# The down product of a hybrid decoder layer: 18 of its 22 features by seven block products in place of eight

## The chip, the cores and the metric

One core of a Trainium2 chip runs the whole layer in one launch. The metric is the device time in microseconds of one execution; the kernel before and the kernel after are run on the same chip. The five engines of the core work by their own queues: TensorE (PE) multiplies matrices, VectorE (DVE), ScalarE (ACT) and GpSimd (POOL) work element by element, and SyncE (SP) issues nearly all DMAs.

## What is computed

One layer for 1024 prompt tokens and 8 sampling tokens (1032 columns, kept as features x tokens), width 1024, feed-forward width 2816, all in float32:

```
def swiglu(x, w_in, w_out):
    gate, up = jnp.split(x @ w_in, 2, axis=-1)
    return (jax.nn.silu(gate) * up) @ w_out
...
x = x + 0.5 * swiglu(rmsnorm(x, ffn1_norm_g), ffn1_w_in, ffn1_w_out)
mix, ... = token_mix(rmsnorm(x, mix_norm_g), ...)
x = x + mix
x = x + 0.5 * swiglu(rmsnorm(x, ffn2_norm_g), ffn2_w_in, ffn2_w_out)
```

The change is in the product with `w_out` of both feed-forward blocks, here called the down product; that with `w_in` is called the up product.

## The kernel before

Everything is cut into tiles of 128 rows: 8 row tiles of the width, 22 of the feed-forward width (called features, `NF`). Each float32 operand is split into a high part (a cast to fp32r on ScalarE) and a low part (operand minus high part, mostly on VectorE; `split`, L250), and each product is three matmuls: high by high, high by low, low by high (`mm3`, L319).

*Up product* (`ffn_in`, L651). From the fifth feature on (the fourth in the second block) it is done by seven block products in place of eight (Strassen's scheme in Winograd's form): the reduction is halved, gate and up are the two halves of one side, and two column blocks of 258 are the other, for two column halves p. Seven operands of the tokens (`xT`) stay for all features; seven of the weights per feature (`w_ops`, L478) are made from two loads, with four additions on GpSimd, a cast on ScalarE and a subtraction on VectorE each. Results go to `hd` in DRAM.

*Down product* (`ffn_out`, L706). It runs plainly in five groups of features (`KGROUPS`, L37), each over 8 row tiles m and 3 column chunks of 344: `one` (L709) does 3 matmuls per feature into a PSUM bank `mm`, and then VectorE adds half the bank to the row tile `x` (the residual). Hidden tiles come back from `hd` by `h_tile` (L677: a load of 1032 columns, a cast, a subtraction). Weights come through `issue` (L296) into eight reserved slots, which `reserve` (L279) claims in the last feature of the up product. In the last group the order is turned, chunk by chunk, so that the work after it (`last_cb`, the next norm's squares and splits) can start on the first chunk.

*Order.* Of the instructions only those of PE stand in the order in which the code records them; the other engines' are put in order by a scheduler when the kernel is built. All large tiles are taken from 44 slots of 1060 columns (`SLOTS`). Work that is made ahead is written as generators (`builders`): `adv` (L418) lets each take a step after a row tile's chunk or a product, and a generator waits (`room`, L414) while too few slots are free. `need_op` (L514) steps them until the operand exists.

Of the kernel before, what the change touches and what calls it, by code (L numbers as in the profile page):

```python
# [36 lines left out]
KGROUPS = [(0, 4), (4, 4), (8, 6), (14, 4), (18, 4)]  # L37
# [77 lines left out]
class Net:  # L115
    def __init__(self, tc, ctx, io):
# [17 lines left out]
        self.alive = 0  # L134
# [120 lines left out]
    def make_plan(self):  # L255
# [12 lines left out]
        for o, w in zip(out, (io["w_out1"], io["w_out2"])):  # L268
            for f0, g in KGROUPS:
                per = PER[g]  # L270
                o += [(w[m0:m0 + per, :, f0:f0 + g, :].rearrange("m p f c -> p m (f c)"), [per, g * P], None) for m0 in range(0, KT, per)]
# [206 lines left out]
    def w_ops(self, s1, s2, n, out, limit):  # L478
# [4 lines left out]
        r1, r2 = self.bt([P, 2 * n], s="r1"), self.bt([P, 2 * n], s="r2")  # L483
        nc.sync.dma_start(r1, s1)
# [13 lines left out]
        st = self.bt([P, 2 * n], s="ws")  # L498
        tt(st[:, a], r2[:, a], r2[:, b], ALU.add)
# [8 lines left out]
        self.fr(r2)  # L508
        tt(r1[:, b], r1[:, b], st[:, b], ALU.subtract)
        self.fr(st)  # L510
        yield from op(r1[:, b])
        self.fr(r1)

# [137 lines left out]
    def ffn_in(self, xT, hd, tail, head):  # L651
# [3 lines left out]
        for f, ps in steps:  # L655
# [5 lines left out]
            for i in range(7):  # L661
# [12 lines left out]
                if f == NF - 1 and i == 1:  # L674
                    self.reserve()
# [9 lines left out]
    def out_ops(self, hd, get):  # L685

        self.hs, self.xr = [], []

        def gen():
            for f in range(NF):  # L690
                while f > 1 and not self.plan and not self.live:
                    yield False
                yield from self.room(3, 2)
                self.hs.append(self.h_tile(f, hd))
                yield True
                if f == KGROUPS[0][1] - 1:
                    for m in range(KT):
                        yield from self.room(1, 2)
                        x = self.bt(s="x")
                        self.nc.sync.dma_start(x, get(m))  # L700
                        self.xr.append(x)
                        yield True

        self.builders.append(gen())

    def ffn_out(self, last_cb):  # L706
        nc = self.nc

        def one(m, c0, w, whi, wlo, o, f0, g):  # L709
            ps = self.pmm()  # L710
            s = slice(c0, c0 + w)
            for j in range(g):
                ks = slice(o + j * P, o + (j + 1) * P)
                h = self.need_op(self.hs, f0 + j)
                self.mm3(ps, whi[:, ks], wlo[:, ks], h[0][:, s], h[1][:, s], j == 0, j == g - 1)
            x = self.need_op(self.xr, m)
            nc.vector.scalar_tensor_tensor(x[:, s], ps, 0.5, x[:, s], ALU.mult, ALU.add)
            self.adv()

        for f0, g in KGROUPS:  # L720
            per = PER[g]
            if f0 + g < NF:
                for m0 in range(0, KT, per):
                    whi, wlo = self.take()
                    for m in range(m0, m0 + per):
                        for c0, w in CHUNKS:
                            one(m, c0, w, whi, wlo, (m - m0) * g * P, f0, g)
                    self.drop()
            else:
                wide = [(self.bt([P, per * g * P], F32R, "whi"), self.bt([P, per * g * P], F32R, "wlo")) for _ in range(KT // per - 3)]  # L730
                ws = [self.take() for _ in range(3)]
                for t in wide:
                    ws.append(self.extra(*t))
                acc = self.bt(s="acc")
                for c0, w in CHUNKS:
                    for m in range(KT):
                        whi, wlo = ws[m // per]
                        one(m, c0, w, whi, wlo, (m % per) * g * P, f0, g)
                        last_cb(self.xr, m, c0, w, None)
                        self.square(acc[:, c0:c0 + w], m, self.xr[m][:, c0:c0 + w])  # L740
# [6 lines left out]
            for f in range(f0, f0 + g):  # L747
                self.fr(*self.hs[f])
# [1010 lines left out]
```

## Time and profile before

| | us |
|---|---|
| median of 3 runs | 2116.67 (2114.20 to 2116.69) |
| profiled execution, its own time | 2115.43 |
| its span, first to last instruction | 2113.2 |
| first block: head and up product | 8.7 to 509.0 |
| first block: down product | 508.9 to 758.5 |
| token mixing and its output product | 758.4 to 1376.3 |
| second block: head and up product | 1376.2 to 1846.7 |
| second block: down product | 1846.6 to 2098.6 |

The profile is of one execution. A row of the groups gives line, engine, operation, written and read tiles, shapes and count, then the busy time and the mean ns of one, then the idle time of the engine just before them and what ended it. Nearly all element-wise work has line L89, that of a helper that records it, so the tiles tell it apart: `wop` is a weight operand, `xlo`/`hlo`/`lo` are low parts, `sw` is the SwiGLU's tile, `ws` and `r` are sums and raw tiles of weights. In a row by windows the columns are named in its header; PEclk is the clock that TensorE was granted, as a share of full speed. In a row of the timeline the first two numbers are start and duration in us.

### The profile page before, as it was taken

How to read it: one execution, taken by the hardware profiler on the slowest of the kernel's cores; microseconds unless marked ns; L12 is line 12 of the kernel's file. 1: busy time of each engine (PE TensorE's matmuls, PEld its weight loads, DVE VectorE, ACT ScalarE, POOL GpSimd, SP SyncE). 2: the span in 40 equal slices, each digit the busy share in tenths (PEclk: the TensorE clock that was granted, in tenths of full speed). 3: DMA queues.
4: the chain of work that ended last, by engine and by line, in shares of the span. 5: the costliest groups of instructions: out<-in, count | busy, mean ns of one | idle time of the engine just before them, and what ended most of it. 6: DMA issues, size and time to landing. Idle time of an engine off the chain costs nothing.

```text
span 2113.2 us, 37138 instructions
## 1 busy us (share of the span) xinstructions
PE 2024.6 (96%) x15062; PEld 1963.6 (93%) x15062; DVE 1222.1 (58%) x2624; ACT 699.8 (33%) x1491; POOL 594.9 (28%) x517
## 2 busy tenths in 40 slices
PE   7799999999999999999999979999999999999997
PEld 6799999999999998787888869899999999999997
DVE  7755555555533544676977874685555555464335
ACT  5233333333211333545243332443333333331112
POOL 3354444341000131332211111245444444200003
PEclk7999999999999999999999979999999999999999
DMA  4112222227322221211212151221222222552112
GB/s 152 60 58 91 81 73 84 86 71 281 113 68 60 84 81 35 69 45 32 67 46 50 57 181 35 97 70 61 86 81 83 79 81 76 194 195 84 55 41 81
DMA packets 109771, 180.81 MB, mean 86 GB/s; under 512 B 35168, under 2 KB 63744, under 8 KB 109584
## 3 DMA queue, kind: packets, MB, share of 16 engines
q1 hardware_dynamic: 109568, 178.41, 26.6%
q8 instruction: 118, 1.93, 0.4%
q14 instruction: 53, 0.43, 0.1%
q0 software_dynamic: 32, 0.03, 0.0%
HBM read 135.60 MB, written 43.85 MB: 85 GB/s over the span
## 4 chain that ended last, share of the span: by engine, by line
PE 40%; DVE 8%; DMA 1%; issue 1%; SPq 1%; ACT 0%; POOL 0%; DVEq 0%; ACTq 0%; POOLq 0%
PE mm L321 6%; PE mm L322 6%; PE mm L323 6%; PE ps L528 4%; PE ps L530 4%; PE ps L529 4%; PE ps L243 3%; PE mm L528 2%; PE mm L530 2%; PE mm L529 2%; DVE conv L89 1%; DVE inv L89 1%; SPq L102 1%; DVE Tb L89 1%; DVE x L89 1%
## 5 line engine op out<-in xcount | busy, mean ns | idle before, releaser
L528 PE MATMUL ps<-xhi,wop 128*128 128x258 f32 x1480 | 421.0, 284 | 7.4 <-DVE sw L89 7.2
L530 PE MATMUL ps<-xhi,wop 128*128 128x258 f32 x1480 | 419.3, 283 | 0.0
L529 PE MATMUL ps<-xlo,wop 128*128 128x258 f32 x1480 | 419.3, 283 | 0.0
L321 PE MATMUL mm<-hhi,hi 128*128 128x344 f32 x1008 | 322.3, 320 | 0.0
L322 PE MATMUL mm<-hlo,hi 128*128 128x344 f32 x1008 | 322.3, 320 | 0.0
L323 PE MATMUL mm<-hhi,lo 128*128 128x344 f32 x1008 | 321.6, 319 | 0.0
L89 DVE TENSOR_TENSOR wop<-r,wop 128x512 fp32r<-128x512 f32 x185 | 158.5, 859 | 253.9 <-ACT wop L89 239.8
L528 PEld LDWEIGHTS ps<-xhi,wop 128*128 128x128 f32 x1480 | 280.9, 190 | 8.7 <-issue 7.2
L529 PEld LDWEIGHTS ps<-xlo,wop 128*128 128x128 f32 x1480 | 281.9, 191 | 0.0
L530 PEld LDWEIGHTS ps<-xhi,wop 128*128 128x128 f32 x1480 | 281.2, 190 | 0.0
L89 DVE SCALAR_TENSOR_TENSOR x<-mm,x 128x344 f32<-128x344 f32 x240 | 123.3, 515 | 220.0 <-PE mm L323 217.9
L89 ACT CAST hi<-raw 128x1024 fp32r<-128x1024 f32 (+1 forms) x78 | 76.7, 984 | 357.0 <-PE mm L322 327.0
L321 PEld LDWEIGHTS mm<-hhi,hi 128*128 128x128 f32 x1008 | 189.4, 188 | 0.3 <-DVE x L89 0.3
L323 PEld LDWEIGHTS mm<-hhi,lo 128*128 128x128 f32 x1008 | 189.4, 188 | 0.0
L322 PEld LDWEIGHTS mm<-hlo,hi 128*128 128x128 f32 x1008 | 189.3, 188 | 0.0
L89 POOL TENSOR_TENSOR acc<-acc,t 128x344 f32<-128x344 f32 (+1 forms) x50 | 45.5, 911 | 508.2 <-ACT t L89 495.9
L321 PE MATMUL mm<-xnhi,hi 128*128 128x344 f32 x488 | 172.1, 353 | 0.0
L528 PE MATMUL mm<-xhi,wop 128*128 128x258 f32 x592 | 167.5, 283 | 0.0
L530 PE MATMUL mm<-xhi,wop 128*128 128x258 f32 x592 | 167.2, 283 | 0.0
L529 PE MATMUL mm<-xlo,wop 128*128 128x258 f32 x592 | 167.0, 282 | 0.0
L89 ACT CAST wop<-r 128x512 fp32r<-128x512 f32 x185 | 114.7, 621 | 144.6 <-PE mm L530 77.0
L323 PE MATMUL mm<-xnhi,lo 128*128 128x344 f32 x488 | 158.6, 325 | 0.0
(320 smaller groups left out, 4607.5 us busy)
## 6 DMA issues: line engine op xcount, KB each, us to landing
r<-in_w_in SPq DMA_DIRECT2D x86, 512.0 KB, 3.6
hraw<-hd SPq DMA_DIRECT2D x44, 516.0 KB, 5.0
hd<-sw SPq DMA_DIRECT2D x74, 258.0 KB, 2.0
raw<-in_w_out SPq DMA_DIRECT2D x34, 512.0 KB, 4.0
raw<-in_w_mix SPq DMA_DIRECT2D x22, 512.0 KB, 3.6
raw<-in_w_out SPq DMA_DIRECT2D x24, 384.0 KB, 3.2
x<-in_x SPq DMA_DIRECT2D x16, 516.0 KB, 9.0
xd<-x SPq DMA_DIRECT2D x24, 172.0 KB, 1.9
```

The source lines that it names most:

```text
L89: return fn(out, *a, **k)
L102: return self.eng.dma_start(out, src)
L243: self.nc.tensor.matmul(out, lhsT, rhs, start=start, stop=stop)
L321: mm(ps, whi, xhi, start=start, stop=False)
L322: mm(ps, whi, xlo, start=False, stop=False)
L323: mm(ps, wlo, xhi, start=False, stop=stop)
L528: mm(ps, w[:, a], x[0][:, c], start=first, stop=False, skip_group_check=True)
L529: mm(ps, w[:, a], x[1][:, c], start=False, stop=False, skip_group_check=True)
L530: mm(ps, wlo, x[0][:, c], start=False, stop=last, skip_group_check=True)
```

## The change

Features 0 to 17 of the down product are done by seven block products, in three groups of six features (`SGROUPS`, `KG` = 3 features in each half of the reduction). Row tiles go in four pairs; a pair, the two halves of the features and two column blocks of 258 make one scheme of seven products, done for both column halves p. One such pass over 14 products is called a cycle here; a group is four cycles. Each product is nine matmuls of 258 columns (`out_product`). Products are accumulated in three PSUM banks so that after each one VectorE adds half of a bank to one block of `x` (`OUT_BANK`, `OUT_TO`): 14 evictions of 258 columns per cycle.

The operands are made by two generators. `wb_ops` makes seven weight operands of 384 columns per cycle, with four additions on GpSimd; at most four are alive (`B_LIVE`). `h_ops` loads eight raw tiles of 774 columns per group and makes seven hidden operands for each p, in three slots per index: a cast of 774 columns, subtractions of 258 and 516 columns on VectorE, and eight subtractions of 774 columns on GpSimd in all. A group's hidden operands stay through its four cycles and are freed index by index in the last. The last four features are done as the last group was before, with three takes and one wide tile; the slots for that are reserved in the last cycle of the third group, no more in the up product. Both blocks are changed alike; the token mixing is not touched.

The core of the diff (the loops that pass arguments on are left out):

```diff
-KGROUPS = [(0, 4), (4, 4), (8, 6), (14, 4), (18, 4)]
+KG = 3
+SGROUPS = [f * 2 * KG for f in range(3)]
+REST = len(SGROUPS) * 2 * KG
+OUT_BANK = (0, 1, 0, 2, 0, 1, 0)
+OUT_TO = ((0, 0), (1, 1), (0, 1), (0, 0), (1, 1), (0, 1), (1, 0))
+B_LIVE = 4
...
+    def wb_ops(self, s1, s2, n, out, limit):
...
+        def op(x):
+            while self.alive >= limit() or not self.slots:
+                yield False
+            t = self.bt([P, 2 * n], F32R, "wop")
+            self.alive += 1
+            self.split(t[:, a], t[:, b], x)
+            out.append(t)
+            yield True
+
+        yield from op(r1[:, a])
...
+        tt(st[:, a], r2[:, a], r2[:, b], ALU.add)
+        tt(st[:, b], st[:, a], r1[:, a], ALU.subtract)
+        tt(r2[:, a], r1[:, a], r2[:, a], ALU.subtract)
...
-                if f == NF - 1 and i == 1:
-                    self.reserve()
...
+    def h_ops(self, hd, f0, out, more):
...
+        for i in range(7):
+            yield from room(3)
+            ts = [self.bt([P, 4 * HW], F32R, "hop") for _ in range(3)]
+            views = []
+            for p, r in enumerate(raws):
+                t = (0, 0)
+                if i in (1, 2):
+                    tt(r[t], r[(0, 1) if i == 1 else (1, 1)], r[t], ALU.subtract)
+                elif i == 4:
+                    tt(r[0, 1], r[1, 1], r[0, 1], ALU.subtract)
+                elif i == 6:
+                    tt(r[1, 0], r[1, 0], r[t], ALU.subtract)
+                x = r[(t, t, t, (1, 0), (0, 1), (1, 1), (1, 0))[i]]
+                hi, lo = ts[p][:, :n], [ts[p][:, n:], ts[2][:, p * e:(p + 1) * e]]
+                self.nc.scalar.copy(hi, x)
+                f = hi.bitcast(F32)
+                self.nc.vector.tensor_tensor(lo[0], x[:, :HW], f[:, :HW], ALU.subtract)
+                self.nc.vector.tensor_tensor(lo[1], x[:, HW:], f[:, HW:], ALU.subtract)
...
+    def out_product(self, i, w, x, banks):
...
+        for k in range(KG):
+            a, b = w[:, k * P:(k + 1) * P], w[:, (KG + k) * P:(KG + k + 1) * P]
+            mm(ps, a, x[0][k], start=i in (0, 1, 3) and k == 0, stop=False, skip_group_check=True)
+            mm(ps, a, x[1][k], start=False, stop=False, skip_group_check=True)
+            mm(ps, b, x[0][k], start=False, stop=k == KG - 1, skip_group_check=True)
...
     def ffn_out(self, last_cb):
...
+        for hb, wb in zip(self.hb, self.wb):
+            for j, ws in enumerate(wb):
+                banks = [], []
+                for i in range(7):
+                    w = self.need_op(ws, i)
+                    views, ts = self.need_op(hb, i)
+                    for p in range(2):
+                        ps = self.out_product(i, w, views[p], banks[p])
...
+                        nc.vector.scalar_tensor_tensor(x, ps, 0.5, x, ALU.mult, ALU.add)
+                    self.fr(w)
+                    self.alive -= 1
+                    if j == KT // 2 - 1:
+                        self.fr(*ts)
+                        if hb is self.hb[-1] and i == 1:
+                            self.reserve()
+                            self.reserved = True
+                    self.adv(2)
```

How the instructions stand. VectorE in the first down product before, between two row tiles of the first group (`lo` is a weight's low part, `hlo` a hidden tile's for the next group, `x` an eviction):

```order
L89 TENSOR_TENSOR lo_5722<-raw_5719,hi_5721 128x1024
L89 SCALAR_TENSOR_TENSOR x_5527<-mm_5725,x_5527 128x344
L89 TENSOR_TENSOR hlo_5676<-hraw_5673,hhi_5675 128x1032
L89 SCALAR_TENSOR_TENSOR x_5527<-mm_5745,x_5527 128x344
L89 SCALAR_TENSOR_TENSOR x_5527<-mm_5765,x_5527 128x344
L89 TENSOR_TENSOR hlo_5742<-hraw_5739,hhi_5741 128x1032
L89 SCALAR_TENSOR_TENSOR x_5529<-mm_5779,x_5529 128x344
```

VectorE after, in the fourth cycle of the first group, from the first hidden operand of the second group on (`hop_6234` is index 0 for p = 0; `wop` are weight operands):

```order
L95 TENSOR_TENSOR hop_6234<-hraw_5690,hop_6234 128x258
L95 TENSOR_TENSOR hop_6236<-hraw_5690,hop_6234 128x516
L95 SCALAR_TENSOR_TENSOR x_5594<-ps_6219,x_5594 128x258
L95 TENSOR_TENSOR wop_6230<-r_625_6107,wop_6230 128x384
L95 SCALAR_TENSOR_TENSOR x_5596<-mm_6243,x_5596 128x258
L95 TENSOR_TENSOR hop_6235<-hraw_5698,hop_6235 128x258
L95 TENSOR_TENSOR hop_6236<-hraw_5698,hop_6235 128x516
L95 TENSOR_TENSOR wop_6265<-r_624_6106,wop_6265 128x384
L95 SCALAR_TENSOR_TENSOR x_5596<-mm_6254,x_5596 128x258
L95 TENSOR_TENSOR wop_6299<-r_625_6107,wop_6299 128x384
L95 SCALAR_TENSOR_TENSOR x_5594<-ps_6208,x_5594 128x258
L95 TENSOR_TENSOR hop_6268<-hraw_5690,hop_6268 128x258
```

Before, evictions of 344 columns alternate with single long splits; now splits of 258, 516 and 384 columns stand between evictions of 258. Further on in the same queue, where the first cycle of the second group has begun:

```order
L95 TENSOR_TENSOR wop_6375<-ws_6342,wop_6375 128x384
L95 SCALAR_TENSOR_TENSOR x_5432<-ps_6471,x_5432 128x258
L95 TENSOR_TENSOR hop_6421<-hraw_5696,hop_6421 128x258
L95 SCALAR_TENSOR_TENSOR x_5432<-ps_6482,x_5432 128x258
L95 TENSOR_TENSOR hop_6307<-hraw_5698,hop_6307 128x258
L95 TENSOR_TENSOR hop_6308<-hraw_5698,hop_6307 128x516
L95 TENSOR_TENSOR wop_6452<-r_646_6302,wop_6452 128x384
L95 TENSOR_TENSOR hop_6412<-hraw_5694,hop_6412 128x258
L95 TENSOR_TENSOR hop_6414<-hraw_5694,hop_6412 128x516
L95 TENSOR_TENSOR wop_6409<-ws_6342,wop_6409 128x384
```

The last row, `wop_6409`, is the weight operand of index 2 of that cycle, and behind `hop_6234` 46 rows after it stand before PE can take that index.

GpSimd before, from the end of the up product into the first down product (`sw` is the SwiGLU, `acc` the next norm's sum of squares):

```order
L89 TENSOR_TENSOR sw_5371<-sw_5371,t_536_5372 128x258
L89 TENSOR_TENSOR sw_5386<-sw_5386,t_538_5387 128x258
L89 TENSOR_TENSOR sw_5371<-sw_5371 128x258
L89 TENSOR_TENSOR sw_5386<-sw_5386 128x258
L89 TENSOR_TENSOR acc_7321<-acc_7321,t_795_7374 128x344
L89 TENSOR_TENSOR acc_7321<-acc_7321,t_797_7394 128x344
```

GpSimd after, at the place of the two fences of VectorE above (`hraw` are the raw hidden tiles of the second group, `ws` and `r` those of the weights):

```order
L95 TENSOR_TENSOR hraw_5690<-hraw_5692,hraw_5690 128x774
L95 TENSOR_TENSOR hraw_5692<-hraw_5694,hraw_5692 128x774
L95 TENSOR_TENSOR hraw_5698<-hraw_5700,hraw_5698 128x774
L95 TENSOR_TENSOR hraw_5690<-hraw_5694,hraw_5690 128x774
L95 TENSOR_TENSOR hraw_5700<-hraw_5702,hraw_5700 128x774
L95 TENSOR_TENSOR ws_6342<-r_647_6303 128x384
L95 TENSOR_TENSOR hraw_5696<-hraw_5696,hraw_5690 128x774
L95 TENSOR_TENSOR hraw_5698<-hraw_5702,hraw_5698 128x774
L95 TENSOR_TENSOR ws_6342<-ws_6342,r_646_6302 128x384
```

Where GpSimd had nothing to do between the two stages' own work, it now has seven subtractions of 774 columns and two of 384 up to what `wop_6409` is made from.

More of the change, by code (lines that the diff above doesn't have):

```diff
@@ L694, in gen @@
                 self.hs.append(self.h_tile(f, hd))
                 yield True
[L696 to L704, printed above, removed]
+        self.builders += [weights(), hidden()]
+    def out_product(self, i, w, x, banks):
+        if len(banks) <= OUT_BANK[i]:
+            banks.append((self.pmm if OUT_BANK[i] == 1 else self.pps)()[:, :HW])
+        ps = banks[OUT_BANK[i]]
+        mm = self.nc.tensor.matmul
+        for k in range(KG):
[3 more added lines that the diff above has]
+            mm(ps, b, x[0][k], start=False, stop=k == KG - 1, skip_group_check=True)
+            self.tick(HW * 3 / 2.2)
+        return ps
```

161 lines of the change are left out of this document (117 added, 44 removed).

## Prediction

> **What bounds the kernel now.** I read the page first, for which engine is full.
>
> ```profile
> PE 2024.6 (96%) x15062; PEld 1963.6 (93%) x15062; DVE 1222.1 (58%) x2624; ACT 699.8 (33%) x1491; POOL 594.9 (28%) x517
> ```
>
> TensorE is, so a change in its work counts one for one as long as nothing else comes to be waited for. A matmul's duration can't be used for that: 258 columns are listed at 284 ns and 344 columns at 320 ns, but they overlap. What counts is the distance from one start to the next, which the view by windows gives as time over count, in stretches where PE never waits: two of the up product (258 columns) and two of the down product (344 columns).
>
> ```profile
> core 0: us, PE busy (x) PEld busy (x) DVE busy (x) ACT busy (x) POOL busy (x), PEclk, DMA share, GB/s
> 200.00:480.00 280.00, 280.00 (x2335) 280.00 (x2334) 150.34 (x237) 90.49 (x181) 122.94 (x111) 1.00 0.24 77
> 520.00:740.00 220.00, 220.00 (x1400) 220.00 (x1399) 102.38 (x158) 48.46 (x63) 7.48 (x8) 1.00 0.29 91
> 1500.00:1820.00 320.00, 320.00 (x2665) 319.95 (x2664) 171.78 (x271) 102.81 (x207) 141.44 (x128) 1.00 0.25 78
> 1860.00:2080.00 220.00, 219.97 (x1404) 219.69 (x1403) 99.53 (x164) 41.21 (x49) 10.48 (x13) 1.00 0.25 75
> ```
>
> So 280.00/2335 and 320.00/2665 make 120.0 ns for 258 columns, 220.00/1400 and 220.00/1404 make 157 ns for 344. The down product is bound by PE alone: VectorE is busy 46% of it and GpSimd 3%. That cover is what the change spends. What DVE does there now, per down product (groups of the first one):
>
> ```profile
> L89 DVE SCALAR_TENSOR_TENSOR x<-mm,x 128x344 f32<-128x344 f32 x119 | 61.2, 515 | 103.9 <-PE mm L323 101.9
> L89 DVE TENSOR_TENSOR hlo<-hraw,hhi 128x1032 fp32r<-128x1032 f32 x18 | 21.9, 1228 | 4.4 <-ACT hhi L89 4.4
> L89 DVE TENSOR_TENSOR lo<-raw,hi 128x1024 fp32r<-128x1024 f32 x13 | 15.9, 1223 | 3.9 <-ACT hi L89 3.9
> ```
>
> **The change, term by term.** *PE.* Each down product has 1584 matmuls of 344 columns. Now 3 groups x 4 row pairs x 7 products x 2 column halves x 9 make 1512 of 258 columns, and four features are left for 288 of 344. That is 1296 x 157 = 203.5 us against 1512 x 120 = 181.4 us: 22.0 us less per feed-forward block, 44 us for the two, if PE never waits. One product of nine matmuls takes 1.08 us, a cycle (one row pair, 14 products) 15.1 us, a group 60.5 us.
>
> *What has to be made for it.* Prices come from DVE's queue when it is full and from GpSimd's:
>
> ```profile
> 142.78 0.68 DVE L89 TENSOR_TENSOR wop<-r,wop 128x512 fp32r<-128x512 f32 x1
> 143.38 1.22 DVE L89 TENSOR_TENSOR xlo<-x,xhi 128x1032 fp32r<-128x1032 f32 x1
> 144.53 0.42 DVE L89 TENSOR_TENSOR t<-mm,rs 128x258 f32<-128x258 f32 x1
> 144.86 1.22 DVE L89 TENSOR_TENSOR xlo<-x,xhi 128x1032 fp32r<-128x1032 f32 x1
> ```
>
> ```profile
> L89 POOL TENSOR_TENSOR sw<-sw 128x258 f32<-128x258 f32 x74 | 54.5, 739 | 30.4 <-ACT sw L89 30.2
> L89 POOL TENSOR_TENSOR ws<-ws,r 128x512 f32<-128x512 f32 x37 | 47.8, 1293 | 73.3 <-DMA r<-in_w_in 73.0
> L89 POOL TENSOR_TENSOR t<-x,t 128x1032 f32<-128x1032 f32 x4 | 9.6, 2400 | 0.2
> ```
>
> ```profile
> L89 ACT CAST hi<-raw 128x768 fp32r<-128x768 f32 x8 | 6.7, 836 | 54.9 <-PE mm L322 54.9
> ```
>
> On DVE, start to start, 512 columns cost 0.60 us and 1032 cost 1.15, so by the line between them 258 cost 0.33, 384 cost 0.46 and 516 cost 0.60; an eviction of 258 columns from PSUM is 144.53 to 144.86, 0.33. On GpSimd 512 cost 1.29 and 1032 cost 2.40, so 384 cost 1.02 and 774 cost 1.85 (estimates on that line). A group then asks of DVE 28 weight operands x 0.46 = 12.9, 14 hidden operands x 0.93 = 13.0, and 56 evictions x 0.33 = 18.5, in all 44.4 us of 60.5; of GpSimd 16 x 1.02 + 8 x 1.85 = 31.1 us. ScalarE's casts (14 near 0.84, 28 shorter ones) stay under 30 us. On the average everything fits. It does not fit where it has to be done.
>
> *Who shares with whom.* DVE's subtractions with two SBUF operands and GpSimd's take turns:
>
> ```profile
> 123.98 1.29 POOL L89 TENSOR_TENSOR ws<-ws,r 128x512 f32<-128x512 f32 x1
> 125.22 1.75 POOL L89 TENSOR_TENSOR r<-r,r 128x512 f32<-128x512 f32 x1
> 126.93 1.19 POOL L89 TENSOR_TENSOR t<-t,t 128x258 f32<-128x258 f32 x1
> ```
>
> ```profile
> 125.95 1.56 DVE L89 TENSOR_TENSOR wop<-ws,wop 128x512 fp32r<-128x512 f32 x1
> ```
>
> ```profile
> L89 DVE TENSOR_TENSOR wop<-ws,wop 128x512 fp32r<-128x512 f32 x74 | 110.3, 1491 | 17.1 <-ACT wop L89 16.4
> L89 DVE TENSOR_TENSOR sw<-ps,sw 128x258 f32<-128x258 f32 x222 | 92.4, 420 | 31.1 <-PE ps L530 29.8
> ```
>
> The subtraction of 0.68 us begins at 125.95 inside a GpSimd one that ends at 126.97, and ends at 127.51, 0.54 us after it: it waited for the whole of the other. Those that read `ws` just after GpSimd wrote it average 1491 ns. Evictions from PSUM are untouched (420 ns, GpSimd busy or not). I therefore add the two engines' SBUF work where both are queued. That mean of 1491 ns could also be read as two engines at half speed. The Trainium skill ("SBUF — State Buffer", section "Who interferes with whom") states that a VectorE instruction with two SBUF inputs and a GpSimd one that reads SBUF exclude each other for the whole instruction; the row at 125.95 agrees. What the half-speed reading would give is a rival below.
>
> *A group's end.* The 21 hidden operand slots of a group are used in all four cycles and come free only in the last, three per product index. With 44 slots (21, 8 for `x`, 8 for raw hidden tiles, some 7 for weights) the next group's operands can't start earlier, and each is wanted one cycle later. From the first such subtraction (hop_6234, possible when the first cast of 0.84 us follows the cycle's first product) to the weight operand wop_6409, which the next group's third product index needs, there are 17.5 us of PE work: 15.1 plus four products less 1.08 and 0.84. DVE has to do before it, by its order, 13 subtractions of 258, 12 of 516 and 7 of 384 columns, 4.3 + 7.2 + 3.2 = 14.7 us, and GpSimd 7 x 1.85 + 2 x 1.02 = 15.0 us. Added, 29.7 us; some 16 handovers overlap by about 0.1 each (0.54 after the release against 0.60), so 28.4. PE is then 11 us late with none of the 15 evictions between (5.0 us) in DVE's way, and up to 17 with all of them and no overlap at handover. About half stand where GpSimd holds the port anyway: **14 us**. At the second group's end the rows are the same, but three weight operands of the following cycle stand ahead of two that are wanted first (3 x 0.46): 11 to 19, **15 us**.
>
> *The first group.* Its operands are made from 16 us before the up product ends to 11 us after, while GpSimd still has four SwiGLU products (0.74 each). DVE 12 x 0.33 + 12 x 0.60 + 5 x 0.46 = 13.5 us and GpSimd 8 x 1.85 + 4 x 1.02 + 3.0 = 21.9 us make 35.4; less 1.5 for handovers that is 7 us more than the 27. The up product may cover a little more of it, the evictions of `sw` add a little: 4 to 9 us late, **6 us**.
>
> *The rest.* Hidden tiles are loaded after the reserved slots are claimed in the last cycle.
>
> ```profile
> hraw<-hd SPq DMA_DIRECT2D x44, 516.0 KB, 5.0
> ```
>
> These four loads (5.0 us to landing), four casts and four splits of 1.2 us have some 10 us of products over them; SP's queue waits at their slots, with only the projection's first weights behind. Nothing to 2 us. A long wait of PE also lowers its clock:
>
> ```profile
> 147.17 0.36 PE L528 MATMUL ps<-xhi,wop 128*128 128x258 f32 x1 [3.03 <-DVE sw L89]
> ```
>
> ```profile
> 147.20:150.60 3.40, 3.40 (x18) 3.40 (x19) 0.17 (x1) 0.62 (x1) 3.40 (x4) 0.57 0.12 41
> ```
>
> After 3.03 us of waiting for DVE, 18 matmuls ran in 3.40 us where 28 fit: 1.2 us lost. After three long waits that is 0 to 4. For the rest and the clock, 0 to 6, **2 us**.
>
> Sum per block: 6 + 14 + 15 + 2 - 22 = 15 us more, 30 us for the two. The profiled execution took 2115.4 us (span 2113.2), the median is 2116.7; from the median that is **2147 us**. The ends, 26 - 22 and 51 - 22 per block, give 2125 and 2175 for this case.
>
> **Rivals.** *DVE and GpSimd don't meet* (faster): GpSimd's work falls where DVE waits for casts or evictions, so only DVE's own queue counts. Then the group's end takes 14.7 + 5.0 = 19.7 us in 17.5, 2 us late, the second 4, the rest 1: 15 us gained per block, **2087 us**. For it: GpSimd's later subtractions wait for DVE's splits of the same raw tile, so its queue has holes. Against it: DVE is behind from the first operand on. 0.17.
> *They share at half speed* (no change): only half of GpSimd's time during SBUF work on DVE is added, 15 x 0.75 x 0.5 = 5.6 us; with 14.7 and the evictions' 5.0 an end is 8 us late and a block costs 4 + 8 + 9 + 2 = 23 against 22: **2119 us**. The row at 125.95 speaks against it. 0.08.
> *The evictions come too late as well* (much slower): they stand in DVE's queue behind the subtractions, and products 4 to 6 accumulate in a bank that has to be read first, so PE already waits within the last cycle, in many short pieces at the lower clock, and what follows starts late. Waits of 60 us per block, **2193 us**. It decides when most evictions lie outside GpSimd's turns. 0.13.
> The forecast has 0.62.
>
> **Range and chances.** About 0.2%, 4 us, is what a measurement of this kernel can tell from no change. The range leaves out the first rival below, and a part of the last above: 2105 to 2190. Faster 0.19 (the first rival and a little of the second), same 0.07, slower 0.74.
>
> **What would show it.** PE's distances of 120 and 157 ns unchanged. In each down product, waits of PE on DVE's `hop`, `wop` and `x`, crowded into two stretches of 30 us around the change of group and one at the start, and hardly any in the second and third cycles; in those stretches DVE full, GpSimd nearly so, and `hop` subtractions of 516 columns far above 0.7 us. If DVE's subtractions keep their undisturbed length there, or PE waits less than 22 us per down product, the forecast is wrong; if PE waits evenly through all cycles, it is the queue and not the change of group.

## The result and the profile after

| | before | after | difference |
|---|---|---|---|
| median | 2115.43 (2113.77 to 2116.69, 4 runs) | 2178.98 (2176.66 to 2181.17, 4 runs) | +63.5 |
| ratio, 95% interval | | | 1.0301 (1.0283 to 1.0319) |
| profiled execution, span | 2113.2 | 2176.5 | +63.3 |
| first block: head and up product | 8.7 to 509.0 | to 512.4 | +3.4 |
| first block: down product | 249.6 | 276.0 | +26.4 |
| token mixing and its output product | 617.7 | 612.4 | -5.3 |
| second block: head and up product | 470.4 | 479.7 | +9.3 |
| second block: down product | 252.0 | 281.6 | +29.6 |

The change costs 63.5 us where 30 were forecast. 56 of them lie in the two down products. Of the 9.3 us ahead of the second, 2.7 are a wait that the change brings at the up product's end, and 6.5 lie in its norm, where a weight's split now stands in VectorE's queue ahead of the norm's small operations (one wait of 5.7 us at 1408.46); the token mixing, which the change does not touch, is 5 us shorter, by another order of instructions. These last two nearly cancel.

First the page of after, TensorE against the others:

```profile
PE 2015.8 (93%) x15494; PEld 1949.8 (90%) x15494; DVE 1427.9 (66%) x3028; ACT 772.0 (35%) x1667; POOL 802.9 (37%) x661
```

TensorE fell from 96% to 93% of a longer span, VectorE gained 206 us of busy time and GpSimd 208; as will be seen, busy time includes waiting for the other engine. Where TensorE stands still is seen when the first down product is cut at its cycles by the windows (start:end, length, then busy time and count of each engine, PEclk):

```profile
core 0: us, PE busy (x) PEld busy (x) DVE busy (x) ACT busy (x) POOL busy (x), PEclk, DMA share, GB/s
512.40:552.80 40.40, 32.52 (x254) 31.93 (x253) 33.54 (x64) 10.61 (x20) 14.76 (x14) 0.92 0.44 132
552.80:568.00 15.20, 15.20 (x129) 15.20 (x128) 9.67 (x21) 3.50 (x7) 4.33 (x4) 1.00 0.18 53
568.00:630.70 62.70, 51.39 (x381) 50.34 (x380) 54.46 (x91) 21.32 (x35) 30.56 (x20) 0.89 0.30 89
630.70:645.80 15.10, 15.10 (x129) 15.10 (x127) 9.78 (x21) 3.49 (x7) 4.36 (x4) 1.00 0.18 53
645.80:697.30 51.50, 39.58 (x255) 38.43 (x254) 49.38 (x76) 20.34 (x34) 29.68 (x19) 0.80 0.17 54
697.30:742.60 45.30, 45.30 (x380) 45.30 (x379) 31.30 (x60) 14.49 (x20) 7.25 (x7) 1.00 0.40 126
```

A cycle has 126 matmuls (a window also counts the two or three that overlap its edges), 15.12 us at 120 ns. The second, fourth and last stretches hold one, one and three cycles and run at exactly that pace, with a full clock. The first holds two: 40.40 less 30.2 is 10.2 us more than the matmuls need, which is here called late. The third, from the last cycle of the first group on, holds three: 17.3 late. The fifth, the last cycle of the second group and the cycle after it, holds two: 21.3 late. The second block is the same: 11.2, 17.7 and 23.1. What TensorE waited for, by the view of the waits in the first block (total us, times, longest; L827 to L829 are the three matmuls of a product, `ps` and `mm` the banks that they write):

```profile
PE ps L827 <- DVE x L95: 17.3, 8, 3.6
PE mm L829 <- DVE wop L95: 8.3, 2, 4.2
PE mm L827 <- DVE sw L95: 2.9, 1, 2.9
PE ps L829 <- DVE wop L95: 2.6, 2, 1.4
```

All of it is VectorE: banks not yet evicted, weight operands not yet made. The waits add up to 31.1 us of the 48.8 that the three stretches are late; the rest is matmuls at a lower clock, to which a later section comes. VectorE's groups show why, with the shapes apart (count, busy us, mean ns of one), and GpSimd's subtractions of the hidden tiles:

```profile
L95 DVE TENSOR_TENSOR hop<-hraw,hop 128x516 fp32r<-128x516 f32 x84 | 89.8, 1071 | 0.6 <-PE ps L582 0.6
L95 DVE TENSOR_TENSOR hop<-hraw,hop 128x258 fp32r<-128x258 f32 x84 | 75.9, 903 | 9.9 <-ACT hop L95 9.9
L95 DVE SCALAR_TENSOR_TENSOR x<-ps,x 128x258 f32<-128x258 f32 x240 | 98.7, 420 | 45.3 <-PE ps L829 45.0
```

```profile
L95 POOL TENSOR_TENSOR hraw<-hraw,hraw 128x774 f32<-128x774 f32 x48 | 96.2, 2012 | 34.1 <-DVE hop L95 19.4 <-ACT sw L95 7.3 <-ACT wop L95 4.1
```

A split of 258 columns takes 903 ns, longer than the eviction of 258 columns, 420 ns, though both write as much. One stretch at the first change of group shows the turns, VectorE first, then GpSimd:

```profile
571.25 0.41 DVE L95 SCALAR_TENSOR_TENSOR x<-ps,x 128x258 f32<-128x258 f32 x1
571.59 2.15 DVE L95 TENSOR_TENSOR wop<-r,wop 128x384 fp32r<-128x384 f32 x1
573.66 0.41 DVE L95 SCALAR_TENSOR_TENSOR x<-mm,x 128x258 f32<-128x258 f32 x1
574.00 2.36 DVE L95 TENSOR_TENSOR hop<-hraw,hop 128x258 fp32r<-128x258 f32 x2
576.28 0.55 DVE L95 TENSOR_TENSOR wop<-r,wop 128x384 fp32r<-128x384 f32 x1
```

```profile
569.42 1.02 POOL L95 TENSOR_TENSOR r<-r,ws 128x384 f32<-128x384 f32 x1 [3.31 <-DVE wop L95]
571.46 4.01 POOL L95 TENSOR_TENSOR hraw<-hraw,hraw 128x774 f32<-128x774 f32 x2 [1.02 <-ACT wop L95]
```

GpSimd's two subtractions run from 571.46 to 575.47, the first of them to 573.32. The split that VectorE begins at 571.59 ends 0.42 us after that and takes 2.15 us, where the same kind takes 0.55 at 576.28, in a hole of GpSimd's queue; the two that it begins at 574.00 end 0.89 us after GpSimd does. The eviction between them takes its usual 0.41.

### The profile page after: what moved, and what is told of

Same layout as the page of the kernel before. It is cut to its first block, busy times and chain, and to the rows that moved or that the text cites. A ratio compares the mean times of both kernels' runs of the same rounds, so it can differ in the third digit from the quotient of the medians.

```text
span 2176.5 us, 39073 instructions
## 1 busy us (share of the span) xinstructions
PE 2015.8 (93%) x15494; PEld 1949.8 (90%) x15494; DVE 1427.9 (66%) x3028; ACT 772.0 (35%) x1667; POOL 802.9 (37%) x661
## 4 chain that ended last, share of the span: by engine, by line
PE 36%; DVE 11%; DMA 2%; issue 2%; ACT 1%; SPq 0%; POOL 0%; DVEq 0%; ACTq 0%; POOLq 0%
PE ps L580 4%; PE ps L582 4%; PE ps L581 4%; PE mm L327 3%; PE ps L249 3%; PE mm L328 3%; PE mm L329 3%; DVE hop L95 2%; PE mm L580 2%; PE mm L582 2%; PE mm L581 2%; PE ps L827 1%; PE ps L829 1%; PE ps L828 1%; DVE x L95 1%
## 5 line engine op out<-in xcount | busy, mean ns | idle before, releaser
L95 DVE TENSOR_TENSOR wop<-r,wop 128x512 fp32r<-128x512 f32 (+1 forms) x305 | 244.6, 806 | 263.8 <-ACT wop L95 250.9
L95 ACT CAST wop<-r 128x512 fp32r<-128x512 f32 (+1 forms) x305 | 174.5, 578 | 293.1 <-PE mm L582 74.9
L827 PE MATMUL ps<-hop,wop 128*128 128x258 f32 x720 | 214.7, 298 | 34.9 <-DVE x L95 34.0
L829 PE MATMUL ps<-hop,wop 128*128 128x258 f32 x720 | 211.8, 294 | 3.9 <-DVE wop L95 3.9
L828 PE MATMUL ps<-hop,wop 128*128 128x258 f32 x720 | 212.6, 295 | 0.0
L95 POOL TENSOR_TENSOR ws<-r 128x512 f32<-128x512 f32 (+1 forms) x61 | 77.4, 1268 | 298.0 <-DMA r<-in_w_in 132.1
L827 PEld LDWEIGHTS ps<-hop,wop 128*128 128x128 f32 x720 | 145.1, 201 | 38.6 <-issue 18.3
L95 POOL TENSOR_TENSOR lo<-raw,hi 128x1024 fp32r<-128x1024 f32 (+1 forms) x30 | 67.6, 2252 | 298.7 <-ACT hi L95 284.3
L95 DVE TENSOR_TENSOR hop<-hraw,hop 128x516 fp32r<-128x516 f32 (+1 forms) x168 | 158.9, 987 | 10.4 <-ACT hop L95 9.9
L95 DVE TENSOR_TENSOR wop<-ws,wop 128x512 fp32r<-128x512 f32 (+1 forms) x122 | 142.4, 1167 | 27.3 <-ACT wop L95 26.7
L328 PE MATMUL mm<-xnlo,hi 128*128 128x344 f32 x488 | 157.9, 324 | 0.0
```

Source lines behind the costliest of these rows:

```text
L95: return fn(out, *a, **k)
L328: mm(ps, whi, xlo, start=False, stop=False)
L827: mm(ps, a, x[0][k], start=i in (0, 1, 3) and k == 0, stop=False, skip_group_check=True)
L828: mm(ps, a, x[1][k], start=False, stop=False, skip_group_check=True)
L829: mm(ps, b, x[0][k], start=False, stop=k == KG - 1, skip_group_check=True)
```

## Experiments

Differences in us are against the kernel before, timed beside each run on the same chip; the kernel after was timed so in the result above, with +63.5, and not again beside these runs. One caution for all of them: the token mixing and its output product, which no edit touches, took between 609.5 and 622.1 us in the traces of these kernels, by the order of instructions. Differences of under some 10 us are therefore read from the down products and not from the time.

### Who makes the hidden tiles' subtractions

**On VectorE.**

```diff
-        tt = self.nc.gpsimd.tensor_tensor
+        tt = self.nc.vector.tensor_tensor
```

> The eight subtractions of 774 columns per group that make the hidden operands go from GpSimd to VectorE. Theory (bunched work at a change of group, DVE and GpSimd taking turns at SBUF): each of three stretches per block loses 7 x 1.85 = 13 us of GpSimd's turns and gains 7 x 0.88 = 6 us of DVE work, so 7 us less in each of six stretches, with less time at the low clock besides: 2125 to 2145 us against 2179. Rival (only DVE's own queue counts, the turns cost nothing): 6 us more in each stretch, 2205 to 2220 us.

2153.09 us, ratio 1.0178 (1.0132 to 1.0225), +37.3. VectorE's groups now, with the subtractions in its own queue:

```profile
L95 DVE TENSOR_TENSOR hop<-hraw,hop 128x516 fp32r<-128x516 f32 x84 | 62.8, 755 | 0.6 <-PE ps L582 0.6
L95 DVE TENSOR_TENSOR hraw<-hraw,hraw 128x774 f32<-128x774 f32 x48 | 47.4, 994 | 0.7 <-DMA hraw<-hd 0.6
L95 DVE TENSOR_TENSOR hop<-hraw,hop 128x258 fp32r<-128x258 f32 x84 | 45.2, 538 | 8.2 <-ACT hop L95 8.2
```

VectorE has 47.4 us more to do and the kernel is 26 us faster: relieving GpSimd is worth more than that load costs, so the rival is out. The number is above the theory's range: the stretches of the first block are still 7.2, 11.4 and 20.2 us late, with VectorE doing all the work itself.

**Left out**: the six lines of the subtractions are deleted; the products then use raw tiles.

> The eight subtractions of 774 columns per group are left out, so the hidden operands are plain blocks; all else is as in the changed kernel. Theory: a stretch has 13 us less to do, what is left (14.7 of DVE, 2 of GpSimd, up to 5 of evictions in 17.5 us) makes PE 0 to 4 us late; PE waits under 10 us per block instead of 50: 2085 to 2110 us. Rival (only DVE's own queue): nothing changes, 2170 to 2185 us. Rival (the chain from one subtraction to the next is what is late): as the theory; the next run tells these two apart.

2114.07 us, ratio 1.000 (0.998 to 1.002), -1.7. All 65 us that separate after from this kernel come with 48 subtractions. The start is not late at all then (the first three cycles take 45.5 us), the changes of group still are, by 5.0 and 11.4 us in the first block. There TensorE still waits for VectorE, mostly for banks; what VectorE is held up by was not taken apart.

**Put aside**: the same subtractions, written to a spare tile (of bfloat16) that nobody reads.

```diff
-                    tt(r[t], r[(0, 1) if i == 1 else (1, 1)], r[t], ALU.subtract)
+                    tt(self.aside, r[(0, 1) if i == 1 else (1, 1)], r[t], ALU.subtract)
```

(and so the other two lines).

> GpSimd makes the same eight subtractions per group, but into a spare tile that nobody reads, and the hidden operands are plain blocks: GpSimd's work stays, nobody waits for its result. Theory (turns at SBUF): the turns are still taken, PE is late by nearly as much as in the changed kernel, 2150 to 2185 us. Rival (the chain of results from GpSimd is what is late): as with the subtractions left out, 2085 to 2110 us.

2142.03 us, ratio 1.0126 (1.0082 to 1.0171), +26.2: between the two theories, and no clean separation. With nobody waiting for them, the scheduler put the subtractions elsewhere, some into quiet cycles where VectorE has time to lose. The splits of 384 columns from raw weights rose to 873 ns (717 in after), those of 516 hidden columns fell to 884 (1071). It shows that turns exist without a chain, not what share of the price they are.

**Fills in place of subtractions.** GpSimd writes the same tiles, for about as long, but reads nothing from SBUF.

```diff
-        tt = self.nc.gpsimd.tensor_tensor
+        def wr(x):
+            for _ in range(2):
+                self.nc.gpsimd.memset(x, 0.5)
...
-                    tt(r[t], r[(0, 1) if i == 1 else (1, 1)], r[t], ALU.subtract)
+                    wr(r[t])
```

> Each of the hidden tiles' GpSimd subtractions is replaced by two constant fills of the same 774 columns in place, so that GpSimd still stands as a step in the chain (after the cast that reads the tile, before the cast that reads it next), for about as long by the row of the one earlier fill (128 columns in 206 ns), but reads nothing from SBUF. The later products then use other numbers. Theory (turn-taking of operations that both read SBUF is the main price): VectorE's splits keep their undisturbed length except beside the weights' additions, the late time falls to near that of the kernel without subtractions: 2110 to 2135 us, hop subtractions of 516 columns under 0.9 us on average. Rival (the chain through GpSimd, its length and its handovers): 2155 to 2180 us, with splits at their undisturbed length and PE still waiting.

2118.10 us, ratio 1.0024 (1.0008 to 1.004), +6.1. Two fills took 1.49 us where a subtraction took 2.01, which left a doubt; so the same with three:

> As the run with two constant fills in place of each of the hidden tiles' subtractions on GpSimd, but with three: a step is then 2.2 us long by the 747 ns of one fill, longer than the 2.01 us that a subtraction took in the kernel after. The later products use other numbers. Theory (the price of a subtraction is the port that it takes from VectorE, not its length in the chain): within 15 us of the run with two fills, 2113 to 2133 us. Rival (two fills were cheap since they were shorter than the subtraction): 2145 to 2180 us.

2120.27 us, ratio 1.0035 (1.0019 to 1.0051), +7.3. GpSimd's group and VectorE's with three fills:

```profile
L95 POOL MEMSET hraw<- 128x774 f32 x144 | 103.6, 747 | 20.5 <-DMA hraw<-hd 12.3 <-DVE hop L95 4.3 <-ACT wop L95 2.0
```

```profile
L95 DVE TENSOR_TENSOR hop<-hraw,hop 128x516 fp32r<-128x516 f32 x84 | 61.2, 729 | 0.6 <-PE ps L582 0.6
L95 DVE TENSOR_TENSOR hop<-hraw,hop 128x258 fp32r<-128x258 f32 x84 | 45.0, 536 | 13.4 <-ACT hop L95 12.8 <-DMA hraw<-hd 0.6
```

GpSimd is busy on these tiles for 103.6 us against 96.2, and VectorE's splits are as short as with no GpSimd work at all on them (the first rows of the run on VectorE read alike). At the first change of group, GpSimd first:

```profile
572.65 6.93 POOL L95 MEMSET hraw<- 128x774 f32 x10
```

```profile
573.53 0.55 DVE L95 TENSOR_TENSOR wop<-ws,wop 128x384 fp32r<-128x384 f32 x1
574.33 1.02 DVE L95 TENSOR_TENSOR hop<-hraw,hop 128x258 fp32r<-128x258 f32 x2
```

Ten fills run without a pause, and the splits beside them keep their short lengths: 0.55 us as in the hole at 576.28, and 1.02 us for a pair of 258 and 516 columns. Of the 65 us, 56 go with these fills and 9 remain. The 56 are not the reading of SBUF alone, since the fills don't stand at all the steps of the chain: the subtraction of index 4 overwrites a tile that the one of index 1 has to read first, and a fill needs to wait for no such reader, so two of a group's eight steps move out of the burst. For the second group the first of them is this one, 42 us before the last cycle of the first group begins at 556.6:

```profile
514.14 0.74 POOL L95 MEMSET hraw<- 128x774 f32 x1 [0.44 <-DVE hop L95]
```

By the down products the 9 lie at the start, 4.9 and 6.1 us late with three fills against 0.0 and 0.7 without subtractions, where all eight steps still stand close together; at the four changes of group together the two runs differ by under 2 us. The Trainium skill ("SBUF — State Buffer", section "Who interferes with whom") says that a VectorE instruction with two SBUF inputs contends with a GpSimd instruction that reads SBUF and not with one that only writes it; these two runs agree, with 1071 ns beside the reader and 729 beside the writer.

### The changes of group

**One group's operands for all.** Groups two and three use the hidden operands of the first.

```diff
-            for f0, hb in zip(SGROUPS, self.hb):
-                yield from self.h_ops(hd, f0, hb, load_x)
+            yield from self.h_ops(hd, 0, self.hb[0], load_x)
```

(the loops of the products and the freeing follow).

> The second and third group use the hidden operands of the first again, so nothing is made at a change of group (the hidden features 6 to 17 are left out of the product); products, evictions and weight operands are all there. Theory: the waits at both changes of group go, 17 to 23 us each, and the first group's stay: 2090 to 2110 us, with cycles of 15.1 us but for the first two. Rival (the seven-product form with 14 evictions and a bank read after each product is slow in itself): cycles stay long wherever they were, 2150 to 2180 us.

2103.54 us, ratio 0.994 (0.9908 to 0.9972), -12.3. The windows of the first block, from the start and from its third cycle on:

```profile
515.70:556.20 40.50, 33.17 (x254) 32.33 (x254) 37.42 (x70) 13.55 (x26) 17.23 (x16) 0.92 0.26 82
556.20:707.60 151.40, 151.40 (x1263) 151.40 (x1262) 96.47 (x206) 38.87 (x69) 37.64 (x35) 1.00 0.24 75
```

Ten cycles run without a gap (1260 x 120 ns = 151.2 us) while 28 weight operands per group and all evictions are still made. The waits at both changes of group are gone, the start stays 10.3 us late (12.5 in the second block). So the two changes cost 75.8 us in the two blocks, and weights and evictions without hidden operands nothing after the second cycle.

**The same without the subtractions**: the six lines are deleted here as well.

> Groups two and three use the hidden operands of the first group, and the hidden tiles' subtractions on GpSimd are left out, so that no change of group and none of these subtractions is left; TensorE does all its matmuls. The output is then another. Theory (the products themselves are worth 22.0 us per feed-forward block, and all else that was lost lies in the making of the hidden operands): before less 44 us, 2066 to 2078 us. Rival (part of the loss is in the products themselves, by their weights or evictions): 2085 to 2103 us.

2084.44 us, ratio 0.9852 (0.9815 to 0.9889), -28.5. The theory's 44 us were not reached: the first two cycles were still 5.5 and 7.3 us late, waiting for evictions.

```profile
510.50:546.10 35.60, 31.85 (x253) 31.49 (x253) 29.91 (x58) 11.99 (x25) 13.65 (x13) 0.95 0.31 94
546.10:697.50 151.40, 151.40 (x1262) 151.40 (x1262) 96.94 (x206) 38.87 (x69) 36.93 (x35) 1.00 0.24 75
```

Added up, 28.5 and 12.8 make 41.3 of 44: the products are worth what the count of matmuls says, to within 3 us.

**Fewer evictions**: only after products 3 and 6.

```diff
-                        nc.vector.scalar_tensor_tensor(x, ps, 0.5, x, ALU.mult, ALU.add)
+                        if i in (3, 6):
+                            nc.vector.scalar_tensor_tensor(x, ps, 0.5, x, ALU.mult, ALU.add)
```

> Of the seven evictions per pair and column half only those after products 3 and 6 are made (five block sums of seven are left out of the output); all operands are made. Theory: DVE loses 10 x 0.33 = 3.3 us per cycle, of which half stood in its way, and PE no longer waits at a bank: 2 to 4 us less in each of six stretches, 2150 to 2168 us; the waits move from x to hop and wop. Rival (the late evictions are what PE waits for in the last cycle of a group): these waits, 8 to 9 us in five cycles, go: 2115 to 2135 us.

2172.00 us, ratio 1.0292 (1.0262 to 1.0321), +61.3. TensorE's waits around the first change of group, 560 to 635 us, in this kernel and then in after:

```profile
PE mm L829 <- DVE wop L95: 6.9, 1, 6.9
PE ps L829 <- DVE wop L95: 4.9, 1, 4.9
```

```profile
PE ps L827 <- DVE x L95: 7.2, 3, 2.6
PE mm L829 <- DVE wop L95: 4.1, 1, 4.1
```

11.8 us against 11.3: the wait for an evicted bank, in the last cycle of the group, became a wait for a weight operand in the cycle after it. Which instruction TensorE is seen to wait for is where the backlog surfaces, not what it consists of. The windows of the first block in this kernel, two cycles each (30.2 us), at the start, the first change and the second:

```profile
511.60:552.20 40.60, 34.35 (x254) 32.88 (x253) 26.83 (x44) 10.55 (x20) 14.41 (x14) 0.92 0.43 131
567.40:614.00 46.60, 34.80 (x254) 34.39 (x253) 39.03 (x49) 17.55 (x28) 25.72 (x16) 0.85 0.34 103
644.30:690.60 46.30, 34.12 (x254) 33.62 (x254) 44.77 (x54) 20.07 (x34) 29.70 (x19) 0.85 0.19 54
```

The first change is 16.4 us late, hardly less than in after (17.3), the second 16.1 in place of 21.3; in the second block it is 16.3 for 17.7 and 16.2 for 23.1. So the evictions cost nearly nothing at the first change and make the second one longer than the first. Over all six stretches it is 17 us less, 2.8 each, which is what the theory said, though not spread as it said. The time shows little of it, since the token mixing and its output product took 9 us longer here (621.5 us) than in after. The rival is out: the waits at the banks went, and most of the lateness stayed.

### The halved clock, and the second change

**Filler in the cycles before and after a change of group**: `out_product` gets three more matmuls with zero weights per product (the zero tile and the argument `more` are added).

```diff
+            for _ in range(more if k == KG - 1 else 0):
+                mm(ps, self.zero, x[0][k], start=False, stop=False, skip_group_check=True)
...
-                        ps = self.out_product(i, w, views[p], banks[p])
+                        ps = self.out_product(i, w, views[p], banks[p], 3 if j == 0 or j == 3 and hb is not self.hb[-1] else 0)
```

> Three more matmuls of zero weights (258 columns, they add nothing to the bank) in each product of the first and last cycles of a group, but for the last cycle of the third: six cycles waiting or next to waiting, 14 x 3 x 0.12 = 5.0 us each, 25 us of PE work per block in five cycles that waited, 5 in one that didn't. Theory (DVE and GpSimd set the pace in these cycles, PE has time to spare): the work goes into the waits, 2165 to 2195 us. Rival (the halved clock, which makes PE's matmuls in these cycles 15 us longer per block, costs time of its own): PE busier keeps its clock, 2145 to 2165 us. Rival (PE's own work sets the pace there): 50 to 60 us more, 2230 us and over.

2192.72 us, ratio 1.039 (1.036 to 1.042), +82.1. The filler was 420 matmuls (15914 against 15494 on the pages), 50.4 us at 120 ns and not the 60 of a first count, and cost 18.6: inside the theory's range and above the clock rival's. Most of the filler took the place of waits. TensorE did keep its clock better: summed from the starts, its matmuls lost 6 and 5 us per block to the lower clock, against some 15 and 17 in after; no gain came of it that the time shows.

**Filler in the first cycle of each group alone** (`3 if j == 0 else 0`):

> Three more matmuls with zero weights per product in the first cycle of each group alone: 252 matmuls, 30.2 us of TensorE work in all, put where the chip granted half the clock after the waits. Theory (TensorE is late by what VectorE and GpSimd have still to do; a halved clock only fills time that would be waited for): the filler takes the place of waits in the two cycles after a change of group and of some in the first, so 30.2 us of work cost 0 to 10 us: 2175 to 2190 us. Rival (the halved clock costs time of its own, some 4 to 6 us at each change of group): 2150 to 2168 us, since the filler keeps the clock up there. Rival (TensorE is not late in those cycles): 2205 us and over.

2196.63 us, ratio 1.0391 (1.037 to 1.0413), +84.6: 30.2 us of filler cost 21 (13 of them in the down products), more than the theory's 10, and the run is slower and not faster than after, as the clock rival would have it. Taken with the run before, 20.2 us of filler in the last cycles of a group cost nothing (the down products of the two runs are alike to within 1 us), and of the 30.2 in the first cycles a bit more than half is hidden. In the cycle after a change TensorE's own progress frees the slots that the next weights are loaded into, so delaying TensorE there may delay what it waits for; that reading was not tested. Nor did this filler keep the clock up: matmuls at half speed still took 13 and 12 us more per block than at full speed. So the run does not measure the clock's price. The trace of after does so in part. TensorE's rows at the first change of group:

```profile
594.87 0.42 PE L828 MATMUL ps<-hop,wop 128*128 128x258 f32 x1
595.08 0.33 PE L829 MATMUL ps<-hop,wop 128*128 128x258 f32 x1
...
595.62 0.28 PE L827 MATMUL mm<-hop,wop 128*128 128x258 f32 x1
595.74 0.28 PE L828 MATMUL mm<-hop,wop 128*128 128x258 f32 x1
600.08 0.58 PE L829 MATMUL mm<-hop,wop 128*128 128x258 f32 x1 [4.06 <-DVE wop L95]
```

```profile
600.10:603.50 3.40, 3.40 (x16) 3.40 (x17) 3.40 (x9) 0.87 (x3) 0.91 (x1) 0.50 0.10 11
```

Up to 595 the starts are 0.21 us apart, at half the clock; faster, TensorE would only have come sooner to the wait of 4.06 us. Behind 600.08 the clock is 0.50 for 3.4 us and no wait follows in that cycle, so there the lost time counts. Summed from the starts behind the last wait of each of the three stretches it is about 5 us in the first block and 6 in the second, of some 15 and 17 in all.

**Three weight operands made ahead in place of four** (`B_LIVE = 3`), for the second change, which in after is longer than the first:

> At most three weight operands are made ahead in place of four. Theory (the second change of group is longer than the first, 21 to 23 us against 17 to 18, since weight operands of the following cycle are queued ahead of hidden operands that are wanted first): the second change falls to that of the first, 2165 to 2175 us. Rival (a weight operand less in hand costs as much in other cycles): 2178 to 2200 us.

2199.55 us, ratio 1.0407 (1.0385 to 1.0429), +87.5. The theory falls: the first change was 21.4 us late (10.0 of it in the cycle after), the second 24.3 in the first block, the start 14.4. Fewer weights in hand cost everywhere. What the traces show at the second change beside that is a late weight load. In the run with two fills GpSimd, at the second change, stands

```profile
639.79 1.05 POOL L95 TENSOR_TENSOR ws<-r 128x384 f32<-128x384 f32 x1
647.33 1.25 POOL L95 TENSOR_TENSOR ws<-ws,r 128x384 f32<-128x384 f32 x1 [6.48 <-DMA r<-in_w_out]
```

6.48 us for the second of two raw weight tiles, whose load was issued at 644.22 where the first's was at 636.54. In after the two loads were issued at 670.12 and 680.33, and GpSimd waited for the second for 0.52 us. Why the second's slot came free so late was not followed further, and no run removed that wait alone.

No kernel that computes the layer came out faster than before, and without any of the subtractions it is just level; so no further version was run.

## Why the prediction was right in its causes and short by half in size

**TensorE's 22 us per block: right.** 45.3 us for three cycles is 120 ns a matmul, and the run without changes of group and subtractions gives the 44 us back to within 3.

**Turn-taking on SBUF: right, and it is the main price.** 56 of 65 us go when GpSimd writes without reading; how many of them are owed to the two steps that left the burst was not measured. On VectorE itself the same subtractions cost 26 us less, for all their load there. The rival that the two don't meet is out by the rows at 571.46; the half-speed rival as well, since the split begun at 571.59 waited for the whole of a GpSimd subtraction.

**The rival of the late evictions** (2193 us, waits of 60 us per block) came nearer in number than the forecast, and TensorE did wait for banks within the last cycle of a group. But with five of seven evictions left out the first change was still 16.4 us late. At the second change the rival has a part of the truth: 5 and 7 us went there.

**Where it is late: right.** Two changes of group and one start, and the quiet cycles at 15.1 us. Of the engines at the first change only VectorE was full; GpSimd, said to be nearly so, was busy for 20.8 of 32.0 us:

```profile
568.00:600.00 32.00, 20.82 (x148) 19.97 (x146) 31.26 (x42) 13.65 (x20) 20.77 (x12) 0.87 0.29 87
```

**How late: too small at the start and at both changes**, in us per block:

| term | forecast | first block | second block |
|---|---|---|---|
| start, with the end of the up product | 6 (4 to 9) | 13.1 | 13.9 |
| first change of group | 14 (11 to 17) | 17.3 | 17.7 |
| second change of group | 15 (11 to 19) | 21.3 | 23.1 |
| rest and clock | 2 (0 to 6) | 0.6 | 2.8 |
| sum | 37 | 52.3 | 57.5 |

Less 22 per block the sums are 30 and 35 us. That is more than the upper ends of the forecast's terms give together, 51 - 22 = 29 (2175 us in all): 2179 lies within the range of 2105 to 2190 only by what was added for the last rival. Before's own down products were 0.9 and 3.3 us longer than their 1584 matmuls at 157 ns, so the last four features bring nothing new; with the second norm and the mixing this comes to the 63.5 measured but for about 1 us. The failed steps are these, the start and the second change first of all.

*The start.* The sentence that "the up product may cover a little more of it" was the wrong way round. The hidden operands' splits stand in VectorE's queue ahead of the up product's own evictions, so they make TensorE wait before the down product has begun. VectorE's rows there:

```profile
503.44 2.30 DVE L95 TENSOR_TENSOR hop<-hraw,hop 128x516 fp32r<-128x516 f32 x1
505.66 0.41 DVE L95 TENSOR_TENSOR sw<-mm,sw 128x258 f32<-128x258 f32 x1
506.00 0.41 DVE L95 TENSOR_TENSOR sw<-ps,sw 128x258 f32<-128x258 f32 x1
```

The split of 516 columns took 2.30 us beside GpSimd, and TensorE's matmul at 506.46 waited 2.89 us for the second of the evictions behind it. That is the 13.1 less the 10.2 of the down product's first cycles. Without the subtractions neither was there (the first three cycles took 45.5 us). With three fills the wait at 506.46 was gone and the first two cycles were 4.9 and 6.1 us late. So some 8 us of the 13.1 and 13.9 go when GpSimd's steps don't read, and some 5 come with the steps themselves. Why the sum of the two queues, 7 us, came out so much smaller is not shown.

*The first change.* 17.3 and 17.7 lie just over the upper end of 11 to 17. In each block 3 us of that (2.8 and 2.7) are matmuls at the lower clock behind the wait at 600.08 and its like, which the forecast had in another line; without them it is 14.5 and 15.0 against 14. That it fits so well is in part luck. "About half stand where GpSimd holds the port anyway" added 3 us for evictions to 11 without any. With most evictions left out, the change was 16.4 us late in place of 17.3: nearly all of them were hidden, and the two queues with the few left, without the clock, made TensorE some 14 us late and not 11. GpSimd's subtractions took 2.01 us on average (1.83 the shortest) and not 1.85, which is 1.1 us over seven. And the wait that ends last is for the operand of product index 1, and not for `wop_6409` of index 2, up to which the forecast had added.

*The second change.* The three weight operands said to be queued ahead were priced at 1.4 us; it is 4.0 and 5.4 longer than the first. With most evictions left out it is no longer than the first, so the surplus goes with evictions that the forecast took to be hidden as at the first change. It doesn't need the hidden tiles' subtractions: it is longer by 6.4 and 6.6 in the run without any (by 2.2 in the first block with three fills). How the evictions bring it about, and what the late weight load has to do with it, stays open.

*The clock.* 2 us for the clock and the rest stood against about 5 and 6 that count behind the last waits; these are inside the rows of the table above, not in its last line, and so explain part of their excess. Whether the other 10 us per block at half speed cost anything stays open.

## What to carry to other kernels

A share of busy time says nothing about a burst: 44 of 60 us of VectorE's work per group fitted on the average, and weights and evictions did fit without a gap, but whatever can only start when a buffer comes free at the end of a stage arrives all at once and has to be priced against the one cycle it has. Where VectorE subtracts two SBUF tiles, work on GpSimd that reads SBUF is not free help in such a burst: here it was cheaper on VectorE itself. What is queued for the next stage also delays what the present stage has behind it in the same queue, and a wait has a second price in the slower matmuls behind it: both belong in the row of the wait.

## What the runs showed of the hardware

GpSimd's constant fills left VectorE's splits at 729 ns, where its subtractions, busy for less time, made them 1071. The same 774-column subtraction took 994 ns on VectorE and 2012 on GpSimd (1834 the shortest). After a wait of 4.06 us the clock stood at 0.50 for some 3.4 us, so waits of 2 to 4 us every few microseconds keep TensorE at half speed for most of the time between them (0.21 us from start to start from the wait at 589.98 to 595): something that the rows around a change of group show and that 0.80 over a whole stretch only hints at.
